# FFN gate and up by seven block products: a two-layer decoder step on one Trainium2 core

## The chip, the core and the metric

The kernel runs on one core of one Trainium2 chip (trn2). The metric is the device time of one execution in microseconds; a run is compared with other runs by the median. The engines are named as in the profile: PE is TensorE (matmul), PEld its weight loads, DVE is VectorE, ACT is ScalarE, POOL is GpSimd, SP is SyncE, whose queue here only issues DMAs.

## What is computed

One step of two layers over 1024 prompt tokens and 8 sample tokens (T = 1032 token columns), model width 1024, all in float32. Each layer is a token mixer (layer 0 an mLSTM, layer 1 a latent attention with a paged cache), an output projection added to the residual, and a SwiGLU FFN added to the residual; a last norm ends it. The part that the change touches:

```python
hp = hp + yp                                   # yp = (...) @ w_out, the output projection
hp = hp + swiglu(rmsnorm(hp, norm_ffn[layer]), ffn_w_gate_up[layer], ffn_w_down[layer])

def swiglu(x, w_gate_up, w_down):              # w_gate_up (1024, 2*2816), w_down (2816, 1024)
    g, u = jnp.split(x @ w_gate_up, 2, axis=-1)
    return (jax.nn.silu(g) * u) @ w_down
def rmsnorm(x, g):
    return x * lax.rsqrt(jnp.mean(x * x, axis=-1, keepdims=True) + EPS) * g
```

## The kernel before

Features lie on the 128 partitions and tokens along the free dimension, so an activation of width 1024 is a tile of 8 feature tiles (KT) by 1032 columns, cut into three chunks of 344 (CW). Every float32 operand of a large product is split into two float32r parts, high and low (`split`, L95: ScalarE copies the high part, VectorE or GpSimd subtracts it for the low one), and one product is three matmuls, high by high, high by low, low by high (`mm3`, L114). A weight block of 128 output features is loaded and split by `load_w` (L120), which has two raw tiles `wr` and two tiles each for the high and low part; `linear` (L138) then runs the three chunks, 8 contraction tiles and 3 terms each: 72 matmuls of 344 columns.

The instructions of each engine are put into an order when the kernel is built, by a scheduler that takes what is ready, earlier program lines first; at run time an engine works through its own list and waits on semaphores. SP's queue holds nearly all loads and stores in such an order, GpSimd's queue a few DMAs beside its arithmetic.

`out_proj` (L723 on) reads the residual X from DRAM (`x_d`) into one tile of 8 x 1032, and for each of 8 output tiles d adds the product of the projection to X and prepares the FFN's operands at once: X times the norm's gain, split, into `xz`, and the squares summed into `rs` (`prep`, L193). The 1/rms of a token is not yet in them. The first gate tile's products (`lead`) run while `rs_of` (L207) makes 1/rms.

`ffn` goes over 22 feature tiles f of the hidden width 2816 in groups of 5, 5, 4, 4, 4. For each f it runs the gate product and the up product, 144 matmuls of 344 columns; `ev_g` (L757) multiplies the gate by 1/rms on VectorE, takes Silu on ScalarE and multiplies by 1/rms again on GpSimd; `ev_u` (L764) multiplies and splits the activation (`ah`, `al`). After a group, the down product of its 4 or 5 tiles is added into X on chip, output tile by output tile (L779 to L786). In layer 0 the last group's down product also prepares the operands of the attention's projections (`to_mla` in `run`); in layer 1 `finish` (L1371) runs the last group's down product in three token ranges, transposes the rows and normalises them to the output. X stays on chip from `out_proj` to the end of the FFN.

The operands of the two projections, `z`, are made by `mlstm` (end, L436 to L444) and by `mla_out` (L1343) and `attention` (L1253 to L1255), each in three chunks of 344 columns.

Of the kernel before, what the change touches and what calls it, by code (L numbers as in the profile page):

```python
# [18 lines left out]
P = 128  # L19
# [11 lines left out]
NCK = S // L  # L31
QL = 384
# [5 lines left out]
# columns of the constant table  # L38
# [34 lines left out]

class Kern:
# [19 lines left out]
    # one exact split of a float32 array into two float32r parts  # L94
# [11 lines left out]
    # the same from PSUM, the low part on GpSimd  # L106
# [7 lines left out]
    def mm3(self, ps, wh, wl, xh, xl, start, stop):  # L114
        mm = self.nc.tensor.matmul
        mm(ps, wh, xh, start=start, stop=False)  # L116
        mm(ps, wh, xl, start=False, stop=False)  # L117
        mm(ps, wl, xh, start=False, stop=stop)  # L118
# [18 lines left out]
    # emit(c, columns, product) for each token chunk of x  # L137
# [10 lines left out]
    # few weight columns: both parts of w side by side, the low one from row o on  # L148
# [17 lines left out]
    # products whose results are used later, so that they run ahead  # L166
# [5 lines left out]
    # 1/sqrt(v) of a small tile: a first guess from the exponent, then Newton steps  # L172
    def rsqrt(self, pool, v, shape, tag):
        V = self.nc.vector
        y = self.t(pool, shape, tag + "y")
        u = self.t(pool, shape, tag + "u")
        V.tensor_scalar(y.bitcast(I32), v.bitcast(I32), 1, None, op0=ALU.logical_shift_right)
# [14 lines left out]
    # x*g split for one feature tile and chunk, and its squares  # L192
# [13 lines left out]
    # rs holds sums of squares per partition on entry, 1/rms on exit  # L206
# [14 lines left out]
    # ---------------------------------------------------------------- set-up  # L221
# [41 lines left out]

    def new_z(self, pool):
# [59 lines left out]
        # 1/rms per token, then as a row on every partition  # L324
# [18 lines left out]
    def mlstm(self, xz, rs, early):  # L343
# [11 lines left out]
        # gates: input gate rows at 0, forget gate rows at 32  # L355
# [42 lines left out]
        # sigmoid(o) * g = tanh(o / 2) * g / 2 + g / 2; the last term is added where it is used  # L398
# [37 lines left out]
        z = self.new_z(self.zp)  # L436
        pz = self.pool("mz")
        for c in range(NCH):
            cs = slice(c * CW, (c + 1) * CW)
            for h in range(8):  # L440
                og = self.t(pz, [P, CW], "og", bufs=6)
                nc.sync.dma_start(og, o_d[:, h, cs])
                nc.vector.scalar_tensor_tensor(og, og, self.gcol(self.G_HEAD + h), v[:, h, cs], op0=ALU.add, op1=ALU.mult)
                self.split(z[0][:, h, cs], z[1][:, h, cs], og, lo_eng=nc.gpsimd if h % 3 == 2 else None)  # L444
# [4 lines left out]
    def gates(self, p1, pg, gi, lf, bcol):  # L449
# [5 lines left out]
        # log sigmoid  # L455
# [4 lines left out]
        # sample gates kept  # L460
# [49 lines left out]
    # one chunk of four heads, as two parts: products, then norm and output  # L510
    def mlstm_chunk(self, pi, c, hg, q, k, v):
# [12 lines left out]
        # decay weights [s, t] per head  # L524
# [11 lines left out]
        # k with its weights, and [v | 1], token major  # L536
# [31 lines left out]
        # state  # L568
# [17 lines left out]
        # h / max(|den|, exp(-m)), then its norm, as one factor per token and head  # L586
# [17 lines left out]
    def mlstm_sample(self, pi, q, k, v):  # L604
# [35 lines left out]
        # weighted k, masked q: [p, b, hp]  # L640
# [5 lines left out]
        # normaliser  # L646
# [20 lines left out]
        # v rows  # L667
# [45 lines left out]
    # out projection into the residual, with the operands of the norm after it  # L713
    def out_proj(self, w, z, gbase, last=False):
        nc = self.nc
        if not last:
            self.fz = self.pool("fz")
        self.xpool = self.pool("xp")
        X = self.t(self.xpool, [P, KT, T], "x")
        self.nt = self.pool("nt")  # L720
        if last:
            self.fz = self.pool("fz")
        xz = self.new_z(self.fz)  # L723
        rs = self.t(self.fz, [P, T], "rs")
        for d in range(KT):
            (nc.gpsimd if last else nc.sync).dma_start(X[:, d], self.x_d[:, d])
# [9 lines left out]
        if last:  # L736
            self.p2.release()
# [772 lines left out]
```

## Time and profile before

| what | us |
|---|---|
| median of 3 runs | 2821.42 |
| lowest and highest run | 2818.59, 2833.71 |
| the profiled execution's span | 2830.2 |
| layer 0: mLSTM, to the first projection product | 0 to 432 |
| layer 0: projection, then FFN | 432 to 538, 538 to 1284 |
| layer 1: attention | 1284 to 1978 |
| layer 1: projection, then FFN | 1978 to 2070, 2070 to 2765 |
| last products and norm | 2765 to 2830 |

The profiled execution is one execution of its own, taken by the hardware profiler; its span is the time from its first to its last instruction. Busy time of TensorE is the union of matmuls that overlap, each some 0.3 us long, so the cost of one matmul in a stream is read from the spacing of the starts. The granted clock in the windows is a share of full speed (2.4 GHz).

### The profile page before, as it was taken

How to read it: one execution, taken by the hardware profiler on the slowest of the kernel's cores; microseconds unless marked ns; L12 is line 12 of the kernel's file. 1: busy time of each engine (PE TensorE's matmuls, PEld its weight loads, DVE VectorE, ACT ScalarE, POOL GpSimd, SP SyncE). 2: the span in 40 equal slices, each digit the busy share in tenths (PEclk: the TensorE clock that was granted, in tenths of full speed). 3: DMA queues.
4: the chain of work that ended last, by engine and by line, in shares of the span. 5: the costliest groups of instructions: out<-in, count | busy, mean ns of one | idle time of the engine just before them, and what ended most of it. 6: DMA issues, size and time to landing. Idle time of an engine off the chain costs nothing. (4 is left out here: it accounts for less than half of the span.)

```text
span 2830.2 us, 47930 instructions
## 1 busy us (share of the span) xinstructions
PE 2720.3 (96%) x19623; PEld 2555.6 (90%) x19623; DVE 1340.7 (47%) x2989; ACT 876.7 (31%) x2021; POOL 721.6 (25%) x729
## 2 busy tenths in 40 slices
PE   8998899999999999999879999999999999999998
PEld 8988888999999999999866666767999999999998
DVE  4366675423222223247668787778432223232324
ACT  4222234321211111243455555655321121212122
POOL 1001232230311121232334444442222120302023
PEclk9999899999999999999989999999999999999999
DMA  5132434111111121122567665663311111111112
GB/s 180 38 75 64 122 108 148 46 40 55 49 38 53 38 60 37 54 87 75 159 204 243 209 230 199 214 237 125 105 46 40 55 40 54 42 53 38 54 41 86
DMA packets 281840, 271.53 MB, mean 96 GB/s; under 512 B 18857, under 2 KB 258990, under 8 KB 273302
## 3 DMA queue, kind: packets, MB, share of 16 engines
q1 hardware_dynamic: 262854, 167.81, 20.0%
q0 software_dynamic: 18000, 98.56, 10.1%
q8 instruction: 154, 2.52, 0.4%
q10 hardware_dynamic: 768, 2.11, 0.3%
q14 instruction: 64, 0.52, 0.1%
HBM read 229.36 MB, written 36.97 MB: 94 GB/s over the span
## 5 line engine op out<-in xcount | busy, mean ns | idle before, releaser
L116 PE MATMUL sc<-zh,wh 128*128 128x344 f32 x2000 | 642.8, 322 | 5.5 <-ACT zh L99 4.9
L117 PE MATMUL sc<-zl,wh 128*128 128x344 f32 x2000 | 641.4, 321 | 1.2 <-DVE zl L100 0.6
L118 PE MATMUL sc<-zh,wl 128*128 128x344 f32 x2000 | 641.1, 321 | 1.1 <-DVE wl L100 1.1
L99 ACT ACTIVATE wh<-wr 128x1024 fp32r<-128x1024 f32 (+3 forms) x219 | 196.8, 899 | 731.0 <-PE mm L117 721.0
L116 PE MATMUL mm<-zh,wh 128*128 128x344 f32 x1192 | 385.4, 323 | 0.5 <-DVE ot L402 0.5
L116 PEld LDWEIGHTS sc<-zh,wh 128*128 128x128 f32 x2000 | 377.2, 189 | 9.1 <-ACT zh L99 5.1
L117 PE MATMUL mm<-zl,wh 128*128 128x344 f32 x1192 | 384.1, 322 | 0.4 <-POOL zl L100 0.4
L118 PE MATMUL mm<-zh,wl 128*128 128x344 f32 x1192 | 383.8, 322 | 0.0
L117 PEld LDWEIGHTS sc<-zl,wh 128*128 128x128 f32 x2000 | 376.8, 188 | 2.9 <-DVE zl L100 1.8
L118 PEld LDWEIGHTS sc<-zh,wl 128*128 128x128 f32 x2000 | 377.5, 189 | 1.8 <-DVE wl L100 1.6
L762 POOL TENSOR_TENSOR sg<-g,rs 128x344 f32<-128x344 f32 x132 | 144.8, 1098 | 782.0 <-ACT g L760 762.3
L100 DVE TENSOR_TENSOR wl<-wr,wh 128x1024 fp32r<-128x1024 f32 (+3 forms) x216 | 224.8, 1042 | 54.2 <-ACT wh L99 51.2
L100 POOL TENSOR_TENSOR al<-sg,ah 128x344 fp32r<-128x344 f32 x132 | 146.5, 1111 | 334.1 <-ACT ah L99 334.1
L117 PEld LDWEIGHTS mm<-zl,wh 128*128 128x128 f32 x1192 | 225.3, 189 | 2.4 <-issue 1.2
L116 PEld LDWEIGHTS mm<-zh,wh 128*128 128x128 f32 x1192 | 225.8, 189 | 1.3 <-DVE ot L402 0.8
L118 PEld LDWEIGHTS mm<-zh,wl 128*128 128x128 f32 x1192 | 225.8, 189 | 0.5 <-issue 0.5
L116 PE MATMUL sc<-ah,wh 128*128 128x344 f32 (+2 forms) x664 | 212.4, 320 | 0.0
L117 PE MATMUL sc<-al,wh 128*128 128x344 f32 (+2 forms) x664 | 212.2, 320 | 0.0
L118 PE MATMUL sc<-ah,wl 128*128 128x344 f32 (+2 forms) x664 | 212.1, 319 | 0.0
L1287 DVE STREAM_TRANSPOSE tt<-nat 128x1024 f32<-128x1024 f32 x128 | 156.4, 1229 | 15.1 <-PE ss L1291 10.2
L760 ACT ACTIVATE g<-g 128x344 f32<-128x344 f32 x132 | 64.4, 488 | 274.0 <-DVE g L759 273.0
L99 ACT ACTIVATE ah<-sg 128x344 fp32r<-128x344 f32 x132 | 64.3, 487 | 269.6 <-DVE sg L765 268.8
(470 smaller groups left out, 4717.9 us busy)
## 6 DMA issues: line engine op xcount, KB each, us to landing
wr<-in_ffn_w_gate_up_dram SPq DMA_DIRECT2D x88, 512.0 KB
wr<-in_mlstm_w_in_dram SPq DMA_DIRECT2D x24, 512.0 KB
wr<-in_ffn_w_down_dram SPq DMA_DIRECT2D x48, 256.0 KB
wr<-in_ffn_w_down_dram SPq DMA_DIRECT2D x32, 320.0 KB
q<-qn_d SPq DMA_DIRECT2D x32, 256.0 KB
qn_d<-qx SPq DMA_DIRECT2D x16, 344.0 KB
x_d<-x POOLq DMA_DIRECT2D x1, 4128.0 KB
o_d<-ot POOLq DMA_DIRECT2D x24, 172.0 KB, 4.6
```

The lines of the kernel that those rows point to most:

```text
L99: ins = nc.scalar.activation(hi, src, AF.Copy)
L100: e.tensor_tensor(lo, src, hi.bitcast(F32), op=ALU.subtract)
L116: mm(ps, wh, xh, start=start, stop=False)
L117: mm(ps, wh, xl, start=False, stop=False)
L118: mm(ps, wl, xh, start=False, stop=stop)
L760: nc.scalar.activation(g1, g1, AF.Silu)
L762: nc.gpsimd.tensor_tensor(sg[c], g1, rs[:, cs], op=ALU.mult)
L1287: V.transpose(out=tt, in_=src.rearrange("p s (c i) -> p c s i", i=32))
```

## The change

Gate and up of one f are taken as one product of a 2 x 2 block matrix. Weight blocks: a11, a12 are the even and odd contraction tiles of the gate's 128 columns, a21, a22 those of the up's. The tokens are cut into two halves of 512 and 520 columns (i = 0, 1), and each half into two blocks of 256 or 260 columns (PW); the even and odd feature tiles of a half by its two blocks are b11, b12, b21, b22. Seven block products (a variant of Strassen's scheme with 15 additions) replace the eight of the plain product. `PRODUCTS` lists them as (product, PSUM bank, first use of the bank): two banks take a second product by accumulation, the other sums are made when a bank is read.

`forms` makes the seven operands of a token half out of X: the 1/rms (`rms_tok`, `as_row`), X times gain times 1/rms in place, the four differences, and seven splits. `operands` makes the seven weight operands of an f: GpSimd adds, ScalarE and VectorE split 512 columns each. `gate_up` runs each product for both halves and evacuates. X is not kept: `out_proj` writes the residual to `x_d`, and `down` adds the down product of two f at a time to `x_d` with accumulating DMAs from GpSimd's queue (`accum_op`), out of a staging tile `st` with two buffers. Its chunks are drawn one by one between the products of `gate_up`. The projection runs for the first token half over all 8 output tiles (512 columns), then for the second (two pieces of 260), with its weights loaded for each; the first half's forms are drawn in while the second half runs. `to_mla` and `finish` read X from `x_d` again and do the last four f's down product.

```diff
+PW = (256, 260)
+PRODUCTS = ((0, "a", 1), (1, "b", 1), (4, "a", 0), (2, "c", 1), (5, "b", 0), (3, "d", 1), (6, "c", 0))
+BANK = {"a": "sc", "b": "sc", "d": "sc", "c": "mm"}
 def out_proj
-        X = self.t(self.xpool, [P, KT, T], "x")
+        X = [self.t(self.xpool, [P, KT, 2 * PW[i]], f"x{i}") for i in range(2)]
+        for i in range(2):
+            for d in range(KT):
+                wh, wl = self.w0 if layer and i == d == 0 else self.load_w(self.wsrc(w, 0, KT, d * P, P), KT, P)
+                m = 512 if i == 0 else PW[1]
+                for c0 in range(0, n, m):
+                    for k in range(KT):
+                        self.mm3(ps, wh[:, k], wl[:, k], zh[:, k, cs], zl[:, k, cs], k == 0, k == KT - 1)
+                    V.tensor_tensor(x, x, ps, op=ALU.add)
...
+                nc.sync.dma_start(self.x_d[:, d, cols[i]], X[i][:, d])
+                next(gen, None)
+            if i == 0:
+                self.zp0.release()
+                self.nf = self.pool("nf", side="right")
+                gen = self.forms(i, X[i], SS, self.G_FFN + 8 * layer)
...
+        for _ in self.forms(1, X[1], SS, self.G_FFN + 8 * layer):
+            pass
+def forms(self, i, X, SS, g0):
+        y = self.rms_tok(SS, n)
+        yield
+        self.as_row(y, rs, n)
+        B = X.rearrange("p (k r) (c t) -> p r c k t", r=2, c=2)
+        def normed(r):
+            for k in range(r, KT, 2):
+                V.scalar_tensor_tensor(X[:, k], X[:, k], self.gcol(g0 + k), rs, op0=ALU.mult, op1=ALU.mult)
...
+        normed(0)
+        put(0, B[:, 0, 0])
+        t1 = sub(B[:, 0, 1], B[:, 0, 0])
+        put(1, t1)
+        yield
+        normed(1)
+        put(4, B[:, 1, 0])
+        yield
+        put(2, sub(B[:, 1, 1], B[:, 0, 1]))
+        yield
+        t2 = sub(B[:, 1, 1], t1)
+        put(5, sub(t2, B[:, 1, 0]))
+        yield
+        put(3, t2)
+        put(6, B[:, 1, 1])
+def operands(self, wg, f):
...
+        G = nc.gpsimd.tensor_tensor
+        G(s, a21, a22, op=ALU.add)
+        G(s3, a11, a21, op=ALU.subtract)
+        yield put(a11)
+        yield put(s)
+        yield put(a12)
+        yield put(s3)
+        yield put(a22)
+        G(s, s, a11, op=ALU.subtract)
+        yield put(s)
+        G(s, s, a12, op=ALU.subtract)
+        yield put(s)
+def gate_up(self, wg, f, parts, down=iter(()), skip=0):
+        for (s, bank, first), w in zip(PRODUCTS, self.operands(wg, f)):
+            for i in parts:
+                for k in range(4):
+                    self.mm3(ps, w[:, 0, k], w[:, 1, k], xh[:, k], xl[:, k], bool(first) and k == 0, k == 3, ...)
+                if s == 0:
+                    nc.scalar.copy(u[:, 1], ps)
+                elif s in (1, 2, 3):
+                    V.tensor_tensor(u[:, 1], u[:, 1], ps, op=ALU.add)
+                elif s == 4:
+                    nc.scalar.activation(g[:, 0], ps, AF.Silu)
+                if s == 3:
+                    V.tensor_tensor(u[:, 0], u[:, 1], banks[i, "b"], op=ALU.subtract)
+                    V.tensor_tensor(u[:, 0], u[:, 0], g[:, 0], op=ALU.mult)
+                if s == 6:
+                    V.tensor_tensor(g[:, 1], u[:, 1], ps, op=ALU.subtract)
+                    nc.scalar.activation(g[:, 1], g[:, 1], AF.Silu)
+                    V.tensor_tensor(u[:, 1], u[:, 1], g[:, 1], op=ALU.mult)
+                    self.split(o(ah), o(al), u, lo_eng=nc.gpsimd)
+                if skip:
+                    skip -= 1
+                else:
+                    next(down, None)
+def down(self, wd, f0):
+        for d in range(KT):
+            raw = self.t(fp, [P, 2, P], "dr", bufs=2)
+            nc.sync.dma_start(raw, self.wsrc(wd, f0 * P, 2, d * P, P))
+            self.split(wh, wl, raw)
+            st = self.t(fp, [P, T], "st", bufs=2)
+            for c in range(NCH):
+                ps = self.tp()[:, :CW]
+                for j in range(2):
+                    self.mm3(ps, wh[:, j], wl[:, j], ah[:, cs], al[:, cs], j == 0, j == 1)
+                nc.scalar.copy(st[:, cs], ps)
+                if c == NCH - 1:
+                    nc.gpsimd.dma_start(self.x_d[:, d], st, accum_op=ALU.add)
+                yield
+def ffn(self, layer):
+        self.gate_up(wg, 0, (0,))
+        self.gate_up(wg, 1, (0, 1))
+        self.gate_up(wg, 0, (1,))
+        for f in range(2, NF - 2, 2):
+            g = self.down(wd, f - 2)
+            self.gate_up(wg, f, (0, 1), g, 4)
+            self.gate_up(wg, f + 1, (0, 1), g)
...
+        self.gate_up(wg, NF - 2, (0, 1))
+        for parts in ((0,), (1,)) if layer else ((0, 1),):
+            self.gate_up(wg, NF - 1, parts)
```

## Rows read from the trace of the kernel before

**Rows 1.** The table of cores: span and granted clock.
```profile
core 0: 2830.2 us, clock 0.983
```
**Rows 2.** The page, part 1: busy us, share of the span, instructions.
```profile
PE 2720.3 (96%) x19623; PEld 2555.6 (90%) x19623; DVE 1340.7 (47%) x2989; ACT 876.7 (31%) x2021; POOL 721.6 (25%) x729
```
**Rows 3.** Windows by stage: from:to, us, busy (instructions) by engine, PEclk, DMA share, GB/s.
```profile
core 0: us, PE busy (x) PEld busy (x) DVE busy (x) ACT busy (x) POOL busy (x), PEclk, DMA share, GB/s
437.00:538.00 101.00, 98.87 (x614) 96.51 (x614) 54.48 (x88) 39.21 (x74) 25.20 (x25) 1.00 0.34 109
538.00:562.00 24.00, 24.00 (x152) 22.64 (x151) 11.40 (x21) 7.82 (x14) 7.37 (x7) 1.00 0.15 45
562.00:1240.00 678.00, 678.00 (x4310) 678.00 (x4309) 189.56 (x298) 124.65 (x202) 138.28 (x125) 1.00 0.16 46
1985.00:2072.00 87.00, 87.00 (x559) 86.37 (x558) 37.95 (x54) 29.53 (x54) 21.01 (x21) 1.00 0.24 78
2072.00:2085.00 13.00, 13.00 (x80) 12.34 (x79) 7.57 (x18) 5.74 (x11) 3.44 (x4) 1.00 0.14 42
2085.00:2700.00 615.00, 615.00 (x3912) 615.00 (x3912) 175.53 (x274) 110.77 (x178) 122.51 (x111) 1.00 0.16 47
```
**Rows 4.** Timeline, VectorE in FFN 1: start us, us, instruction; first gate chunk, successive f.
```profile
2699.49 0.52 DVE L759 TENSOR_TENSOR g<-sc,rs 128x344 f32<-128x344 f32 x1 [1.61 <-PE sc L118]
...
2722.13 0.52 DVE L759 TENSOR_TENSOR g<-sc,rs 128x344 f32<-128x344 f32 x1 [1.61 <-PE sc L118]
```
**Rows 5.** Timeline, TensorE in the tail: first and last of 21 matmuls, two widths.
```profile
2796.73 0.34 PE L116 MATMUL sc<-ah,fw 128*128 128x384 f32 x1
...
2800.24 0.33 PE L118 MATMUL sc<-ah,fw 128*128 128x384 f32 x1
...
2812.92 0.28 PE L116 MATMUL sc<-ah,fw 128*128 128x264 f32 x1
...
2815.37 0.28 PE L118 MATMUL sc<-ah,fw 128*128 128x264 f32 x1
```
**Rows 6.** Groups by form, VectorE: form xcount, busy us, mean ns, idle before.
```profile
L100 DVE TENSOR_TENSOR wl<-wr,wh 128x1024 fp32r<-128x1024 f32 x130 | 160.7, 1236 | 46.2 <-ACT wh L99 46.2
...
L100 DVE TENSOR_TENSOR wl<-wr,wh 128x512 fp32r<-128x512 f32 x42 | 29.1, 693 | 0.2
...
L100 DVE TENSOR_TENSOR wl<-mm,wh 128x256 fp32r<-128x256 f32 x32 | 12.9, 403 | 2.1 <-ACT wh L99 1.8
L181 DVE TENSOR_TENSOR fu<-fu,ssq 128x4 f32<-128x4 f32 x48 | 9.3, 194 | 1.5
...
L1416 DVE SCALAR_TENSOR_TENSOR yo<-sc,r,gB 128x512 f32<-128x512 f32 x7 | 5.2, 748 | 0.1
```
**Rows 7.** Groups by form, ScalarE.
```profile
L760 ACT ACTIVATE g<-g 128x344 f32<-128x344 f32 x132 | 64.4, 488 | 274.0 <-DVE g L759 273.0
...
L99 ACT ACTIVATE wh<-wr 128x512 fp32r<-128x512 f32 x43 | 27.2, 633 | 158.5 <-PE mm L117 158.2 <-ACT rs L200 0.3
...
L1204 ACT COPY ot<-mm 128x256 f32<-128x256 f32 x28 | 10.4, 371 | 40.9 <-PE mm L1201 40.9
```
**Rows 8.** Groups by form, GpSimd.
```profile
L112 POOL TENSOR_TENSOR wl<-spl,wh 128x512 fp32r<-128x512 f32 x43 | 54.8, 1284 | 41.0 <-ACT spl L111 39.3 <-issue 1.1
```
**Rows 9.** Line 726, loads of x on GpSimd's queue: issue ns, landing us min/median/max.
```profile
L726 POOL DMA_DIRECT2D x<-x_d x8: 550/558/612, 1978.4 to 1982.1; - x8
...
DMA to landing us min/median/max: 4.8/9.8/10.9
```
**Rows 10.** Timeline, VectorE and GpSimd at the end of projection 0.
```profile
527.46 0.57 DVE L103 SCALAR_TENSOR_TENSOR zl<-x,g,zh 128x344 fp32r<-128x344 f32 x1 [0.65 <-ACT zh L102]
...
531.90 1.12 POOL L204 TENSOR_TENSOR rs<-rs,sq 128x344 f32<-128x344 f32 x1 [3.07 <-ACT sq L203]
...
532.14 1.24 DVE L103 SCALAR_TENSOR_TENSOR zl<-x,g,zh 128x344 fp32r<-128x344 f32 x1
```
**Rows 11.** Timeline, TensorE's first projection product in layer 0, idle before it.
```profile
432.30 0.66 PE L116 MATMUL sc<-zh,wh 128*128 128x344 f32 x1 [4.88 <-ACT zh L99]
```

More of the change, by code (lines that the diff above doesn't have):

```diff
@@ L71, in host_tables, with __init__, __getitem__ @@
     return c, r.astype(np.float32)
+class Stack:
+    def __init__(self, tiles):
+        self.tiles = tiles
+    def __getitem__(self, ix):
+        return self.tiles[ix[1]][:, ix[2]]
 class Kern:
@@ L219, in rs_of, with rms_tok, as_row @@
             nc.scalar.copy((rs if out is None else out)[:, j * QW:(j + 1) * QW], ps)
+    def rms_tok(self, SS, n):
+        nc = self.nc
+        c, rem = divmod(n, P)
+        ps = self.tp()
+        for i in range(c):
+            nc.tensor.matmul(ps[:, i:i + 1], SS[:, i * P:(i + 1) * P], self.ones[:, 0:1], start=True, stop=True)
+        v = self.t(self.gp, [P, 9], "tv")
+        w = c + (rem > 0)
+        if rem:
+            nc.gpsimd.memset(v[:, c:w], 1.0)
+            nc.tensor.matmul(ps[:rem, c:w], SS[:, c * P:n], self.ones[:, 0:1], start=True, stop=True)
+            nc.vector.tensor_scalar(v[:rem, c:w], ps[:rem, c:w], 1.0 / D, EPS, op0=ALU.mult, op1=ALU.add)
+        nc.vector.tensor_scalar(v[:, :c], ps[:, :c], 1.0 / D, EPS, op0=ALU.mult, op1=ALU.add)
+        return self.rsqrt(self.gp, v[:, :w], [P, 9], "t", w)
+    def as_row(self, y, out, n):
+        for c0 in range(0, n, 512):
+            ps = self.tp()
+            m = min(512, n - c0)
+            for i in range(0, m, P):
+                w = min(P, m - i)
+                t = (c0 + i) // P
+                self.nc.tensor.matmul(ps[:, i:i + w], y[:, t:t + 1].to_broadcast([P, P]), self.ident[:, :w], start=True, stop=True)
+            self.nc.scalar.copy(out[:, c0:c0 + m], ps[:, :m])
     def setup(self):
@@ L262, in gcol, with half_z @@
         return self.g[:, o:o + 1]
+    def half_z(self):
+        self.zp1 = self.pool("z1", side="right")
+        self.zp0 = self.pool("z0", side="right")
+        pools = (self.zp0, self.zp1)
+        return [[self.t(pools[i], [P, KT, 2 * PW[i]], "zh" + str(i) + x, F32R) for x in "hl"] for i in range(2)]
     def new_z(self, pool):
@@ L741, in ffn, with out_proj @@
[L741 removed]
+    def out_proj(self, w, z, layer):
         nc = self.nc
         V = nc.vector
[L744 to L790 removed]
@@ L1388, in finish @@
             W.append(tuple(w[:, i].rearrange("p (k m) -> p k m", m=P) for i in range(2)))
+        for cs in cuts[1:]:
+            for d in range(KT):
+                nc.sync.dma_start(X[d][:, cs], self.x_d[:, d, cs])
         gB = self.t(fp, [P, D], "gB")
@@ L1443, in finish @@
         fp.release()
+        self.fp.release()
+        self.fz.release()
     def run(self):
```

326 lines of the change are left out of this document (201 added, 125 removed).

## The prediction

> **What bounds the kernel now.** I read the table of cores first: one core, a span of 2830.2 us, a granted clock of 0.983 [rows 1]. The page's engine shares put TensorE at 96% and the next engine, VectorE, at 47% [rows 2]; a share over the whole span says little, so the windows by stage come next. In both FFN stretches TensorE is busy for all of the 678 and 615 us, at clock 1.00, VectorE for 28% of them, ScalarE for 18%, GpSimd for 20% [rows 3]. The two projection windows are 98% and 100% TensorE, and even the hand-over from projection to FFN has no gap: 24.0 of 24.0 and 13.0 of 13.0 us [rows 3]. So in the FFN a microsecond of matmul removed is a microsecond of the kernel, as long as no other engine becomes late.
>
> What one matmul costs is read from starts, not from the 0.32 us durations, which overlap. One feature tile of gate and up is 144 matmuls of 344 columns and comes round every 22.64 us [rows 4]: 157.2 ns each. In the tail, 21 matmuls of 384 columns start within 3.51 us and 21 of 264 columns within 2.45 us, each with 20 spacings: 175.5 and 122.5 ns [rows 5]. The line through these two has 0.442 ns per column and 5.9 ns fixed; it gives 157.8 at 344 columns (measured 157.2), 119.0 at 256, 120.7 at 260 and 232 at 512.
>
> **The change, part by part.**
>
> *Gate and up.* Removed: 22 tiles x 144 x 2 layers = 6336 matmuls at 157.2 ns, 996.2 us. Added: 7 products x 2 token halves x 4 contraction tiles x 3 split terms = 168 per tile, 7392 in all, half at 256 and half at 260 columns, mean 119.9 ns: 885.9 us. Net -110.3 us. Bounds: were a matmul strictly proportional to its columns (118 ns) it would be -124; were none under the 122.5 ns of the 264-column row, -91.
>
> *Down.* The same 1584 matmuls per layer, at 344 columns in the same three chunks, now two tiles deep for all but the last four: 0. In the steady loop one step is a product half (12 x 119.9 ns = 1.44 us) and one down chunk (6 x 157.2 = 0.94 us), so a pair of tiles takes 28 x 1.44 + 24 x 0.94 = 63 us. VectorE in a pair: 14 weight splits of 512 at 0.69, 28 small operations on a token half at about 0.42 (between the 0.40 of the 256-column row and 0.52 at 344), 8 splits of 256 at 0.40 [rows 4, 6]: 25 us, 39%. ScalarE: 14 x 0.63, 16 operations of 0.37 to 0.63, 24 copies of 0.49, 8 x 0.37 [rows 7]: 30 us, 48%. GpSimd: 8 sums and 4 splits of 512 at 1.28 [rows 8] and 8 DMA issues at 0.57 [rows 9]: 20 us, 32%. TensorE covers all three, so I book 0, with up to +20 for small waits at the finer hand-overs (three hand-overs where there was one).
>
> *Accumulating DMAs.* Each `down` step of one feature tile ends with a 516 KB accumulate issued by GpSimd; 72 per layer. No row shows an accumulate. The nearest are plain 516 KB reads on the same queue: 4.8 us for the quickest of eight in a burst, 9.8 us in the median, 10.9 us for the slowest [rows 9]. The staging tile `st` has two buffers, so a DMA has from the end of its third chunk to the end of the first chunk two tiles later, four steps, 9.5 us; the two PSUM banks of that helper give two steps more before TensorE itself waits, 14.3 us. An isolated plain transfer (one every 7.2 us here, not eight at once) is nearest to 4.8 us; doubled it is 9.6. Cost 0; what it costs beyond 14.3 us is rival C.
>
> *Hand-over from projection to FFN.* This is where the change pays. Before, gate products ran on unscaled operands while the 1/rms was still being made. Now the second token half needs X, its sum of squares, the 1/rms row, eight scalings, four differences and seven splits before its first product can end. TensorE's cover is the first half's pass of tile 0 (84 x 119 ns = 10.0 us) and then tile 1 with both halves (20.2 us). VectorE's work from the last projection product to the end of tile 1: about 3.4 us in the 1/rms chain (13 small operations at 0.19, two at 0.42), 8 scalings of 520 at 0.75, 11 operations of 1040 at 1.24, 12 weight splits of 512 at 0.69, 19 evacuations at 0.42 [rows 6]: 39 us against 30.2 us of matmul. So TensorE waits for at least 9 us. GpSimd adds to it: a VectorE operation that usually takes 0.57 us took 1.24 beside a GpSimd sum of 1.12 [rows 10], 0.67 more. Eleven GpSimd operations in this stretch, if each costs that once, make 7 us. I take 16 per layer, +32 in all; bounds +10 (work drawn ahead of the hand-over) and +50 (the forms go first on VectorE and the weights starve).
>
> The Trainium skill, "SBUF — State Buffer", section "SBUF: two separate sides", says more: VectorE operations with two SBUF inputs and GpSimd operations hold one port pair in turn, and the loser blocks for the whole instruction. The rows just cited agree in kind. By that rule all 11 x 1.28 = 14 us of GpSimd work would be lost to VectorE, 23 us per layer, and the time would be some 14 us higher (rival B).
>
> *Projection by halves.* 192 matmuls at 232 ns and 384 at 120.7 against 576 at 157.2: 90.9 against 90.5 us, 0. While the second half runs (46 us), VectorE has the first half's forms (8 x 0.75 + 11 x 1.24 = 19.6), 16 residual adds at 0.42 and 8 weight splits at 1.24 (the weights are now loaded twice) [rows 6]: 36 us, plus GpSimd collisions. It fits in sum but comes in lumps of up to 7 us against 5.8 us of matmul; the next weight split stands behind them on VectorE, and TensorE waits for it: +3 per layer, +6 (0 to +16). The first product now needs 512 instead of 344 columns of z from VectorE; before it TensorE already sat idle 4.9 us [rows 11]. Eight times 0.17 us more, scaled up by the splits: +1.5 per projection, +3 (-2 to +6, below nothing as the longer first product covers more). The stores of X go on SP's queue between the weight loads; each waits for a residual add, with the next weight already loaded: 0.
>
> *One-half passes* (tile 0 in two passes in both layers, the last tile in two passes in layer 1): weight forms made once more per 10 us pass, VectorE 7 x 0.69 + 7 x 0.42 = 7.8 us [rows 6], so only collisions can make it late: +4 (0 to +10). *Ends:* reading X back from DRAM before the last products, 3 KB to 4 KB rows on SP's queue among the weights: the last accumulate was issued some 40 us earlier, and reads of tiles other than the last fit under the last pass: +2 (0 to +8). Layer 0's end, with the same matmuls and x read instead of held: +1 (0 to +4).
>
> **Sum.** -110.3 + 32 + 6 + 3 + 4 + 2 + 1 = -62. The profiled execution's own span, 2830.2 us, lies 0.3% over the median of the runs, 2821.4, and inside their 2818.6 to 2833.7; I apply the difference to the median: 2759 us.
>
> **The rivals.**
>
> *A. The hand-overs are hidden.* The forms are drawn ahead and the stalls keep to their low bounds: -110 + 10 + 5 = -95, 2726 us. For it: TensorE has no gap there today [rows 3]. Against: 39 us of VectorE work in 30 us.
>
> *B. VectorE and GpSimd are late.* Each GpSimd operation of the hand-over costs VectorE its whole 1.28 us (14 us on top of the 9), and forms that go first hold back the weights for some 7 more: hand-over 30 per layer, projection 8 per layer by the same collisions, steady loop +10: -110 + 60 + 16 + 10 + 10 (the other small terms) = -14, 2807 us. For it [rows 10]; against, shares of 39% and 32% in the steady loop.
>
> *C. The accumulating DMA becomes the bound: slower.* Place: the `st` buffer in the steady loop. Each us beyond 14.3 delays every second feature tile by one, 72 x 2 / 2 = 72 us over the kernel. It cancels the gain at about 15.2 us, and at twice the median landing of that burst (2 x 9.8 = 19.6 us) it costs +380: about 3140 us; just past the point, at 16.5 us, it gives 2821 - 62 + 158 = 2917. For it: no row prices an accumulate, which reads, adds and writes DRAM. Against: the lone plain landing of 4.8 us [rows 9], the DMA engines only 16% busy in the FFN [rows 3], and 9.5 us until the first effect.
>
> *D. The change does not do what it says:* the pitch at 256 columns sticks at 122.5 ns or above. That is -91 instead of -110, 2778 us, inside the forecast's own range.
>
> **How the numbers follow.** Forecast (with D) 0.51, own range 2738 to 2790; A 0.19; B 0.17; C 0.13. The predicted time is the forecast's, 2759. The range reaches from A's side (gate and up at -110 with low bounds of the rest, about -103: 2718) to beyond B (2815), and leaves out C and the far end of A. A measurement of this kernel can tell about 0.5% from no change, 14 us. Faster by more: the forecast, A and half of B, 0.78. Within: the rest of B, 0.09. Slower: C, 0.13.
>
> **What the profile after would show.** Gate and up right: TensorE matmuls of 256 and 260 columns at a spacing of 119 to 121 ns, 3696 each, and a pair of tiles every 63 us with TensorE full. Hand-over right: TensorE idle 10 to 25 us within the 30 us after the projection's last product in each layer, its waits ended by VectorE (low halves of forms or weights), the clock perhaps falling there. Accumulate right: landings under 10 us, no ScalarE copy to `st` waiting for a DMA. Rival B shows as VectorE near 100% through the second projection half; rival C as gaps of TensorE repeated every 14 us, ScalarE waiting on the DMA of `st`. The forecast is wrong if the steady loop takes more than 66 us a pair, or if the hand-overs cost under 5 or over 25 us each.

## The result, and the profile after

The changed kernel takes 2795.4 us (median of 4 runs, 2784.6 to 2797.4), the kernel before 2826.3 us beside it: ratio 0.988, interval 0.985 to 0.991. That is faster by 1.2%, 31 us, half of the 62 us forecast and inside the range. The profiled execution has a span of 2795.7 us against 2830.2 [rows 1], 34.5 us less.

The page's engine shares after (busy us, share of the span, instructions), and below it the windows by stage (columns as in [rows 3]): the projection of layer 0, four stretches of its FFN, then the same for layer 1.

```profile
PE 2631.5 (94%) x20739; PEld 2446.1 (87%) x20739; DVE 1588.1 (57%) x3542; ACT 1209.0 (43%) x2855; POOL 926.8 (33%) x887
```

```profile
426.90:536.60 109.70, 99.10 (x595) 87.91 (x596) 71.52 (x94) 41.18 (x62) 30.73 (x24) 0.94 0.55 173
536.60:562.00 25.40, 5.60 (x35) 5.31 (x35) 21.05 (x36) 10.65 (x15) 2.58 (x3) 0.58 0.22 62
562.00:580.00 18.00, 16.95 (x124) 16.66 (x124) 12.71 (x21) 8.45 (x17) 8.45 (x6) 0.83 0.15 45
580.00:600.00 20.00, 18.71 (x156) 18.50 (x156) 12.96 (x23) 7.55 (x16) 7.90 (x7) 1.00 0.23 65
600.00:1200.00 600.00, 600.00 (x4612) 600.00 (x4611) 254.69 (x484) 264.37 (x586) 219.52 (x192) 1.00 0.57 114
1941.40:2052.30 110.90, 104.80 (x627) 92.91 (x627) 63.52 (x94) 41.00 (x71) 38.25 (x41) 0.93 0.53 168
2052.30:2080.00 27.70, 6.44 (x37) 5.82 (x37) 23.31 (x37) 10.80 (x15) 1.26 (x1) 0.57 0.19 57
2080.00:2100.00 20.00, 19.38 (x152) 19.38 (x153) 12.85 (x21) 9.91 (x19) 9.72 (x7) 0.91 0.23 65
2100.00:2700.00 600.00, 598.65 (x4599) 598.44 (x4598) 252.78 (x487) 263.95 (x584) 220.24 (x193) 1.00 0.57 115
```

The steady loop is as full as before: 600.0 of 600.0 us. Where [rows 3] had 24.0 of 24.0 in the hand-over from projection to FFN there are now 5.6 of 25.4, at a granted clock of 0.58, with VectorE busy 21.05. The projections, 98% to 100% TensorE before, have holes of 10.6 and 6.1 us.

From here on a projection is the time from its first product on z to the start of its last residual add, and an FFN from there to the first product of what follows (the operands z of layer 1's attention, "MLA" in the code, or the last down product), read from the starts of these instructions. By these marks the projections of the kernel before run from 432.3 to 530.1 and from 1961.9 to 2058.7 us; the table of the kernel before sets their ends and the second one's start later, at 538, 2070 and 1978, but TensorE is just as full between (31.94 of 31.94 us from 530.06 to 562).

| kernel | ratio to before | projection 0 / 1, us | FFN 0 / 1, us |
|---|---|---|---|
| before | 1 | 97.8 / 96.8 | 750.5 / 704.7 |
| changed | 0.988 (0.985 to 0.991) | 109.7 / 110.9 | 719.4 / 679.3 |
| e1_order | 0.987 (0.985 to 0.989) | 111.1 / 115.0 | 718.1 / 675.8 |
| e2_one_form | 0.979 (0.976 to 0.981) | no trace used | no trace used |
| e3_lo_gpsimd | 0.990 (0.988 to 0.993) | 109.5 / 107.7 | 725.2 / 682.7 |
| e4_plain_store | 0.989 (0.987 to 0.991) | 109.4 / 109.4 | 719.1 / 679.3 |
| e5_proj_order | 0.990 (0.988 to 0.993) | 112.7 / 110.4 | 719.1 / 678.7 |
| e7_one_form_both | 0.973 (0.970 to 0.975) | 104.9 / 99.9 | 708.4 / 666.5 |
| e8_eighth_product | 1.031 (1.028 to 1.033) | 111.2 / 108.3 | 779.3 / 737.8 |
| e9_no_gpsimd | 0.990 (0.988 to 0.993) | 112.0 / 113.7 | 719.5 / 679.3 |
| e11_lag | 0.984 (0.982 to 0.986) | 107.8 / 110.2 | 716.3 / 673.8 |
| e14_deep_weights | 0.985 (0.983 to 0.987) | 106.3 / 105.5 | 719.1 / 678.8 |
| e15_lag_deep | 0.983 (0.981 to 0.985) | 105.9 / 107.1 | 715.5 / 673.9 |
| e16_spread_x | 0.979 (0.977 to 0.981) | 101.6 / 105.3 | 716.2 / 672.2 |

The kernel before took 2826 to 2828 us beside e1 to e5, e14 and e15, and 2852 to 2860 us beside e7, e8, e9, e11 and e16, so only ratios and stages are compared across. An FFN that an edit leaves alone repeats within 0.7 us (the changed kernel, e5, e9 and e14: 719.1 to 719.5 and 678.7 to 679.3); a projection left alone scatters by 3 to 4 us (107.8 to 111.2 and 107.7 to 110.9 in the changed kernel, e3, e4, e8 and e11). Of e2 only the times of undisturbed executions are used.

The 34.5 us, stage by stage: FFNs -31.1 and -25.4, projections +11.9 and +14.1, the way to the first projection product -5.4, MLA +4.1, the tail -2.7.

In the hand-over of layer 0, the one long wait of TensorE, and what ScalarE and VectorE did before it (timeline of the changed kernel: start us, us, engine, instruction, idle before and what ended it; L936 copies the first product out of PSUM, L112 and L113 are the high and low parts of a split):

```profile
561.12 0.58 PE L129 MATMUL sc<-f4h,wl 128*128 128x256 f32 x1 [16.71 <-ACT u L936]
...
559.74 1.07 ACT L112 ACTIVATE c5h<-T 128x1040 fp32r<-128x1040 f32 x1 [1.23 <-DVE T L844]
560.72 0.35 ACT L936 COPY u<-sc 128x256 f32<-128x256 f32 x1
...
544.91 3.44 DVE L840 SCALAR_TENSOR_TENSOR x<-x,g,rs 128x520 f32<-128x520 f32 x5 [2.91 <-ACT rs L261]
548.27 1.24 DVE L844 TENSOR_TENSOR T<-x 128x1040 f32<-128x1040 f32 x1
...
561.93 1.24 DVE L113 TENSOR_TENSOR c5l<-T,c5h 128x1040 fp32r<-128x1040 f32 x1
```

TensorE has done one product of tile 0 and needs its copy u to go on; ScalarE makes that copy behind the last of the second half's seven high copies, and these come as VectorE delivers the scaled X and the differences, from 544.9 to 563 us without a gap. So two readings were open: the order is wrong (ORDER: copy and weight splits behind the forms), or VectorE has too much to do (THROUGHPUT).

### The profile page after: what moved, and what is told of

Same layout as the page of the kernel before. It is cut to its first block, busy times and chain, and to the rows that moved or that the text cites. A ratio compares the mean times of both kernels' runs of the same rounds, so it can differ in the third digit from the quotient of the medians.

```text
span 2795.7 us, 52716 instructions
## 1 busy us (share of the span) xinstructions
PE 2631.5 (94%) x20739; PEld 2446.1 (87%) x20739; DVE 1588.1 (57%) x3542; ACT 1209.0 (43%) x2855; POOL 926.8 (33%) x887
## 5 line engine op out<-in xcount | busy, mean ns | idle before, releaser
L971 ACT COPY st<-ss 128x344 f32<-128x344 f32 x432 | 190.5, 441 | 208.4 <-PE ss L131 193.7
L131 PE MATMUL ss<-ah,dl 128*128 128x344 f32 x864 | 277.2, 321 | 0.0
L130 PE MATMUL ss<-al,dh 128*128 128x344 f32 x864 | 276.2, 320 | 0.0
L129 PE MATMUL ss<-ah,dh 128*128 128x344 f32 x864 | 276.0, 319 | 0.0
L112 ACT ACTIVATE wh<-wr 128x512 fp32r<-128x512 f32 (+2 forms) x152 | 119.8, 790 | 223.3 <-PE mm L130 127.2
L973 POOL DMA_DIRECT2D x_d<-st x144 | 125.2, 869 | 228.9 <-ACT st L971 219.3
L113 POOL TENSOR_TENSOR al<-u,ah 128x512 fp32r<-128x512 f32 (+1 forms) x88 | 124.2, 1411 | 156.9 <-ACT ah L112 156.8
L113 DVE TENSOR_TENSOR wh<-S,wh 128x512 fp32r<-128x512 f32 x95 | 84.2, 888 | 159.6 <-ACT wh L112 108.4
L129 PEld LDWEIGHTS ss<-ah,dh 128*128 128x128 f32 x864 | 162.8, 188 | 0.0
L130 PEld LDWEIGHTS ss<-al,dh 128*128 128x128 f32 x864 | 162.5, 188 | 0.0
L131 PEld LDWEIGHTS ss<-ah,dl 128*128 128x128 f32 x864 | 162.3, 188 | 0.0
L113 DVE TENSOR_TENSOR wl<-S,wl 128x512 fp32r<-128x512 f32 x93 | 68.2, 734 | 112.8 <-ACT wl L112 85.8
L1539 PEld LDWEIGHTS ss<-tt,qbd 128*32 128x32 f32 x2560 | 70.8, 109 | 43.3 <-DVE tt L1535 12.8
L113 DVE TENSOR_TENSOR wl<-wr,wh 128x1024 fp32r<-128x1024 f32 (+2 forms) x80 | 88.4, 1109 | 35.3 <-ACT wh L112 32.7
L113 DVE TENSOR_TENSOR dl<-dr,dh 128x256 fp32r<-128x256 f32 x144 | 76.7, 533 | 55.0 <-ACT dh L112 55.0
L129 PE MATMUL mm<-zh,wh 128*128 128x344 f32 x320 | 106.3, 332 | 0.2 <-DVE ot L451 0.2
L131 PE MATMUL mm<-zh,wl 128*128 128x344 f32 x320 | 105.3, 329 | 0.0
```

What stands on the lines that cost most here:

```text
L112: ins = nc.scalar.activation(hi, src, AF.Copy)
L113: e.tensor_tensor(lo, src, hi.bitcast(F32), op=ALU.subtract)
L129: mm(ps, wh, xh, start=start, stop=False, **kw)
L130: mm(ps, wh, xl, start=False, stop=False, **kw)
L131: mm(ps, wl, xh, start=False, stop=stop, **kw)
L971: nc.scalar.copy(st[:, cs], ps)
```

## The experiments

**The hand-over: order, or VectorE.** First the order alone; tile 0's buffers got a pool of their own:

```diff
-        for _ in self.forms(1, X[1], SS, self.G_FFN + 8 * layer):
+        gen = self.forms(1, X[1], SS, self.G_FFN + 8 * layer)
+        self.gate_up(wg, 0, (0,), gen)
+        for _ in gen:
             pass
```

> Only the order of issue is changed, in both layers: the seven first-half products of tile 0, with their weight splits and evacuations, are issued interleaved with the forms of the second half instead of behind them (their buffers lie in a pool of their own). Theory ORDER: the 22 to 25 us that TensorE now stands idle behind the projection are idle because the first copy of a product to SBUF and the weight splits queue on ScalarE and VectorE behind the forms; the half pass (84 products of 0.12 us, 10.1 us) then runs inside that stretch: 10 us less per layer, about 2775 us, and the wait of 16.7 us for the copy u is gone. Rival THROUGHPUT: VectorE has some 22 us of forms to do in any order, and the half pass puts about 11 us more of splits and additions between them; only the 8 us of the 1/rms chain, in which VectorE is half idle, is won: 0 to 7 us per layer, 2782 to 2795 us, with TensorE idle in pieces instead of in one block.

Measured: 2791.1 us, 4 us less, which is inside the scatter of the runs; the FFNs gain 1.3 and 3.5 us, but in the same trace the projections are 1.4 and 4.1 us longer. Windows of layer 0 from the last residual add on:

```profile
540.60:555.00 14.40, 12.47 (x90) 11.96 (x89) 13.17 (x26) 7.22 (x13) 6.79 (x6) 0.88 0.45 137
555.00:575.00 20.00, 2.14 (x17) 1.93 (x16) 18.79 (x24) 9.18 (x11) 0.78 (x1) 0.68 0.03 8
```

The half pass now runs at once, and the hole comes behind it: 17.9 of 20 us, with VectorE at 18.79. The long wait for u is gone and its time is not. This speaks for THROUGHPUT, but its sign (TensorE idle in pieces) is not there, and an order on another engine is not ruled out. The one long wait ends with the split of tile 1's first weights, and in ScalarE's list that split stands behind tile 0's last evacuation, for which ScalarE waits 3.4 us (timeline of e1, TensorE and ScalarE):

```profile
574.71 0.58 PE L129 MATMUL sc<-f0h,wh 128*128 128x256 f32 x1 [17.86 <-ACT wh L112]
...
572.57 0.42 ACT L958 ACTIVATE gt<-gt 128x256 f32<-128x256 f32 x1 [3.38 <-DVE gt L957]
...
574.05 1.13 ACT L112 ACTIVATE wh<-wr 128x512 fp32r<-128x512 f32 x2
```

The next edit gives GpSimd a part of VectorE's work:

```diff
-            self.split(F[s][0], F[s][1], x)
+            self.split(F[s][0], F[s][1], x, lo_eng=nc.gpsimd if i and s in (1, 2, 3) else None)
```

> Three of the seven low parts of the second half's forms are computed by GpSimd instead of VectorE; order unchanged. Theory ORDER: the copy u still stands behind the last high copy, at most 3 us per layer less, 2789 to 2796 us. Rival THROUGHPUT: VectorE loses 3 x 1.4 us of its row of forms and the last high copy comes as much earlier: 4 to 5 us per layer less, 2785 to 2788 us. Rival COLLISION (GpSimd and VectorE slow each other): no gain or a loss, 2795 us or more.

Measured: 2799.8 us; the FFNs lose 5.8 and 3.4 us. Two VectorE operations of 1.24 us beside GpSimd's low parts (timeline, layer 0):

```profile
558.91 3.42 DVE L113 TENSOR_TENSOR f7l<-x,f7h 128x1040 fp32r<-128x1040 f32 x1
562.25 3.41 DVE L844 TENSOR_TENSOR T<-T,x 128x1040 f32<-128x1040 f32 x1
...
558.51 2.71 POOL L113 TENSOR_TENSOR c2l<-T,c2h 128x1040 fp32r<-128x1040 f32 x1 [4.33 <-ACT c2h L112]
561.19 3.37 POOL L113 TENSOR_TENSOR c3l<-T,c3h 128x1040 fp32r<-128x1040 f32 x1
```

Each ends 1.1 us after the GpSimd operation beside it, about its own length: the rows read as if it waited for the end of that one. GpSimd takes 2.7 to 3.4 us for what VectorE does in 1.24, so the trade loses: COLLISION. This is what the Trainium skill, "SBUF — State Buffer", section "SBUF: two separate sides", says of the port pair that VectorE and GpSimd share: the one that starts first holds it for its whole instruction and the other waits. These rows agree with it.

What the forms cost in all was priced by leaving them out (part of the computation: one form stands in for seven; four scalings, four differences and six splits are not done), first in the second half, then in both:

```diff
         put(0, B[:, 0, 0])
+        if i:              # e7: in both halves
+            for s in range(1, 7):
+                F[s] = F[0]
+            return
```

> Leaves out part of the computation: of the second half's seven forms only the first is made, and it stands in for the other six (four normalised tiles, five differences, six splits per layer are not done). It prices the forms of the second half whole. If the missing part of the FFN's gain lies in the hand-over: 18 to 25 us per layer less than the changed kernel, 2745 to 2760 us, and the windows behind the projection fill up. If it lies elsewhere (a longer product, the accumulating DMA, the clock in the steady loop): less than 5 us per layer, over 2785 us.

> Leaves out part of the computation: of the seven forms of both halves of the tokens only the first is made, and it stands in for the other six. Against the run in which only the second half's forms were cut (2760 to 2767 us) it prices the forms of the first half, which are made during the second half of the projection. Theory THROUGHPUT (VectorE has more work than time there, about 18 us of forms beside the weight splits): the gap of 3.6 to 4 us behind the middle of each projection and the stretch at a lower clock behind it are gone, 4 to 6 us per layer less than that run, 2752 to 2758 us. Rival: these gaps come from the weight loads or from the order of the weight splits alone: within 3 us of that run.

Measured: 0.979 and 0.973. Against the changed kernel the second half's forms cost 0.0094 x 2826 = 27 us, 13 per layer, less than the 18 to 25 expected; the first half's another 16 us, 8 per layer, more than the 4 to 6 expected. The intervals of the ratios leave some 10 us either way on both. The stages of e7 say the same: FFNs -11.0 and -12.8, projections -4.8 and -11.0 (against e8's, beside the same runs of the kernel before, -6.3 and -8.4). A window in its second projection half, and then the same window and one in the first half of the changed kernel:

```profile
505.00:525.00 20.00, 20.00 (x170) 20.00 (x169) 8.79 (x13) 8.02 (x13) 8.34 (x8) 1.00 0.41 126
```

```profile
505.00:525.00 20.00, 16.38 (x122) 15.97 (x120) 19.38 (x21) 8.96 (x13) 6.55 (x6) 0.91 0.27 86
440.00:450.00 10.00, 3.02 (x10) 1.81 (x9) 10.00 (x12) 4.61 (x7) 3.05 (x3) 0.76 0.92 289
```

The last edit here takes work off VectorE's path: tile 0 in one pass over both halves, with the second half's products two weight combinations behind and one form issued between, so the second pass with its seven splits falls away:

```diff
-        self.gate_up(wg, 0, (0,))
         self.gate_up(wg, 1, (0, 1))
-        self.gate_up(wg, 0, (1,))
+    def first_tile(self, wg, gen):     # called with forms(1) as gen, ahead of ffn
+        for (s, bank, first), w in zip(PRODUCTS, self.operands(wg, 0)):
+            self.product(s, bank, first, w, 0, banks)
+            self.evacuate(s, bank, 0, banks, 0, U, Gt)
+            next(gen, None)
+            ...                        # product of half 1, two combinations behind
```

> The first tile of gate/up is done in one pass over both halves, issued together with the second half's forms: the second half's product of each weight combination follows two combinations behind the first half's, one form of the second half is issued between them, and tile 0's separate second-half pass, with its reload and splits of the weights, falls away. VectorE's work on the path shrinks by that pass (7 splits of 0.69 us and its additions), and 20 us of products lie beside the 19 us of forms in place of none. If VectorE's throughput is what binds, this should give 8 to 12 us per layer, 2771 to 2779 us; if the latency from form to form and the order on ScalarE bind instead, less than 3 us per layer, 2789 us or more.

Measured: 0.984, the FFNs 3.1 and 5.5 us shorter; half of what was expected, and in neither theory's range. From the last residual add to 600 us TensorE idles 14.9 us where the changed kernel idled 22.1. The edit changes work and order at once, so it does not tell the two apart. The two longest waits that stay, each in both layers, are for the first form and again for the split of tile 1's weights on ScalarE, of the kind that the rival named (timeline of e11, layer 0):

```profile
555.36 0.58 PE L130 MATMUL sc<-c0h,wl 128*128 128x260 f32 x1 [4.30 <-ACT c0h L113]
...
583.88 0.39 PE L130 MATMUL sc<-f0h,wh 128*128 128x256 f32 x1 [3.79 <-ACT wh L113]
```

**The projections.** A first try at order: weights issued ahead of the forms' next piece, finer pieces, the loads of x spread.

```diff
+                w1 = weights(i * KT + d + 1)
                 nc.sync.dma_start(self.x_d[:, d, cols[i]], X[i][:, d])
-                if i == d == 0:
-                    load(1)
+                if i == 0:
+                    (nc.gpsimd if layer else nc.sync).dma_start(X[1][:, d], self.x_d[:, d, cols[1]])
                 next(gen, None)
```

> Only the projections are changed: the weights of a step are split before the forms' next piece is issued and not behind it, the first two steps' weights of layer 0 ahead of the second half of z, the second half of x is loaded one block per step instead of eight blocks at once, and the forms of the first half come in finer pieces. Theory ORDER: the gaps of the two projections (7 and 4 us in layer 0, 2 and 4 us in layer 1, and the stretches at half clock behind them) are weight splits queued on VectorE behind z or forms, and weight loads behind x loads: 8 to 12 us per layer less, 2771 to 2780 us. Rival: VectorE or the DMA engines are full in these stretches whatever the order: less than 3 us per layer, over 2789 us.

Measured: 2800.1 us, no gain. This does not decide against ORDER: the timeline of e5 says that the edit could not act. In layer 0's first half only the first two steps' splits had been put ahead of z, and TensorE waited 5.46 us for the third's, as before. In the second half, weights have two buffers, so the split of a step waits for TensorE to leave the buffer of two steps before, and by then the lump is on VectorE:

```profile
504.81 1.06 ACT L112 ACTIVATE wh<-wr 128x1024 fp32r<-128x1024 f32 x1 [0.60 <-PE sc L130]
...
506.46 2.61 DVE L853 SCALAR_TENSOR_TENSOR x<-x,g,rs 128x512 f32<-128x512 f32 x3
508.99 1.21 DVE L113 TENSOR_TENSOR wl<-wr,wh 128x1024 fp32r<-128x1024 f32 x1
```

Then GpSimd's share of the projections given to VectorE:

```diff
-                self.split(z[i][0][:, h], z[i][1][:, h], og, lo_eng=nc.gpsimd if h % 3 == 2 else None)
+                self.split(z[i][0][:, h], z[i][1][:, h], og)
...
-                        (V if d == KT - 1 else nc.gpsimd).tensor_tensor(SS[:, cs], SS[:, cs], sq, op=ALU.add)
+                        V.tensor_tensor(SS[:, cs], SS[:, cs], sq, op=ALU.add)
... (and the same for the z of layer 1)
```

> In the two projections the low parts of z and the sums of squares that GpSimd computes are given to VectorE; nothing else is changed. Theory COLLISION (VectorE stands still while GpSimd computes, so a low part of 512 columns costs 1.35 to 1.5 us of both where VectorE alone takes 0.69): the stall of 7 us at the start of layer 0's projection shrinks by 3 to 5 us, and layer 1's stages by 1 to 3 us: 2785 to 2791 us. Rival: VectorE is the engine that is full and gets more to do: 2796 to 2803 us.

Measured: 0.990, projections 112.0 and 113.7 us: no gain, as the rival had it. The collisions there cost no more than the work would on VectorE. Then the buffers:

```diff
+        self.w3 = self.pool("w3", bufs=2, side="right")
...
+                while len(Q) <= min(j + (3 if i else 0), 2 * KT - 1):
+                    Q.append(weights(len(Q)))
```

> Only the projections' weights are changed: three steps' weights in layer 0 are split ahead of the second half of z, and in the second half of both projections the weights are split up to four steps ahead in two more pairs of buffers, ahead of the first half's forms. VectorE's work is the same. If the gaps in the projections are lumps (VectorE has enough time over the whole stage, 37 us of work in the 48 us of the second half, but the splits that TensorE needs come behind 20 us of forms), buffers cure them: 5 to 9 us per layer less than the changed kernel, ratio to the kernel before 0.981 to 0.984. If VectorE is full over the whole stage, the gap only moves to the next stage: within 2 us per layer, ratio 0.986 to 0.990.

Measured: 0.985, 9 us less than the changed kernel; projections 3.4 and 5.4 us shorter. The same window of the second half:

```profile
505.00:525.00 20.00, 20.00 (x169) 20.00 (x168) 20.00 (x23) 10.76 (x15) 7.26 (x6) 1.00 0.34 109
```

VectorE is full for all 20 us and TensorE is too. So this gap was a lump and not a lack: the splits lay behind the forms, and buffers cure it. What stays is in the first half (layer 0: TensorE waits 3.9 us for one split, then 2.5 us for another). With both edits that helped (e15), ScalarE waits for a weight in layer 1:

> Both edits that leave VectorE's work on the path smaller or earlier: tile 0 of gate/up in one pass issued together with the second half's forms (ratio to the kernel before 0.984 alone), and the projections' weights split further ahead. If the two gaps are separate lumps of the same engine the gains add: ratio 0.976 to 0.981, faster than both kernels. If VectorE is full over the whole stretch from the projection to the second tile, the second edit brings nothing on top: 0.983 to 0.986.

```profile
1955.16 1.06 ACT L113 ACTIVATE wh<-wr 128x1024 fp32r<-128x1024 f32 x1 [13.09 <-DMA wr<-in_mla_w_o_dram]
```

Measured: 0.983, faster than both kernels. As a ratio this is less than the sum of the two (0.981) and lies in the range for "nothing on top", but by stages the two do add: the FFNs are as short as e11's, the projections, within their scatter, as e14's. The 13.1 us is the wait of ScalarE; TensorE loses 3.2 us of it. The expectation of the next run places that load behind the eight blocks of x. In layer 0 the blocks do stand before the weights in SP's queue, but in layer 1 they go through GpSimd's queue, and the load only runs beside them, with the DMA engines 95% busy or more from 1935 to 1955 us. That expectation's 100.0 us for projection 1 also leaves out its first 7 us; from its first product it takes 107.1. The last run spreads the blocks:

```diff
-                if i == d == 0:
-                    load(1)
+                if i == 0:
+                    (nc.gpsimd if layer else nc.sync).dma_start(X[1][:, d], self.x_d[:, d, cols[1]])
```

> The kernel with the one-pass first tile and the weights split ahead, with one more edit: the second half of x is loaded one block per step of the first half, not eight blocks behind the first step, and the first half's weights are loaded one step further ahead. In the run without it the weight loads of steps 3 and 4 stand behind the eight blocks of x (ScalarE waits 13.1 us for one in layer 1, TensorE stands 2.7 to 3.9 us at a time, the DMA engines over 95% busy). If that queue is the rest of the projections' excess (105.9 and 100.0 us against 97.8 and 96.8 before), each layer gains 2 to 5 us more: ratio 0.980 to 0.982. If VectorE's second half of z is what holds TensorE there, no change: 0.983.

Measured: 0.979 (2798.8 us where the kernel before took 2859.6; interval 0.977 to 0.981), the lowest ratio of a kernel that leaves nothing out: 2.1% faster than before. Projection 0 is 4.3 us shorter than in e15. Projection 1 is 1.8 us shorter, which is inside the scatter, and this was on a chip whose MLA was slower (706 us against 678 in e15, unedited in both), so what the spreading does in layer 1 stays open.

**The two terms taken for certain.** An eighth product, without use:

```diff
                 if s == 0:
+                    px = self.tp()[:, :pw]
+                    for k in range(4):
+                        self.mm3(px, w[:, 0, k], w[:, 1, k], xh[:, k], xl[:, k], k == 0, k == 3, skip_group_check=True)
```

> Adds work without use: in each pass the first block product is computed a second time into a spare bank that nobody reads, so that there are eight products again, with 12 x 2 x 22 x 2 = 1056 more products of 256 or 260 columns. If TensorE sets the pace of the FFN all through, each costs its 0.12 us: 127 us more than the changed kernel, about 2922 us, and seven products in place of eight are worth as much. Rival: in part of the FFN something else sets the pace (VectorE, the accumulating DMAs, the weights' loads) and the added products fall into its idle time: less than 100 us more, under 2895 us.

Measured: 0.0427 x 2826 = 121 us more than the changed kernel; by stages 59.9 and 58.5 us per FFN for 528 matmuls, 111 to 113 ns each. At the forecast's 119.9 ns they would be 63.3 us, so TensorE sets the pace except for 3 to 5 us per FFN; that these fell into the hand-over's hole is likely and not shown. And the store without accumulation (the sums then don't reach the residual):

```diff
-                    nc.gpsimd.dma_start(self.x_d[:, d], st, accum_op=ALU.add)
+                    nc.gpsimd.dma_start(self.dump_d[:, d], st)
```

> Leaves out part of the computation: the DMAs of the down products store them to another place in DRAM in place of adding them to the residual there; same bytes sent, no reading back by the DMA. It prices the accumulation. Theory: the accumulating DMAs are hidden (landing 5.6 us in the median against a budget of 9.5 to 14 us, 11 us of waits for their buffers in the whole run, and those beside a full TensorE): within 8 us of the changed kernel (ratio to the kernel before 0.985 to 0.991). Rival: accumulation slows the weights' loads or holds ScalarE's copies so that it is part of what is missing of the gain: 10 us or more less (ratio under 0.984).

Measured: 0.989, FFNs 719.1 and 679.3 us: the accumulation costs nothing.

## Why the prediction was right or wrong

**Gate and up, -110: right.** Starts of the first and last of 12 matmuls of 256 columns, and of one and the same subtraction in successive pairs of tiles (timelines of the changed kernel, TensorE and VectorE):

```profile
750.93 0.28 PE L129 MATMUL sc<-f3h,wl 128*128 128x256 f32 x1
...
752.23 0.28 PE L131 MATMUL sc<-f3h,wl 128*128 128x256 f32 x1
```

```profile
727.78 0.42 DVE L945 TENSOR_TENSOR gt<-u,mm 128x256 f32<-128x256 f32 x1 [0.54 <-PE mm L131]
...
790.61 0.42 DVE L945 TENSOR_TENSOR gt<-u,mm 128x256 f32<-128x256 f32 x1 [0.54 <-PE mm L131]
```

1.30 us over 11 spacings is 118.2 ns (119.0 from the line through [rows 5]); a pair takes 62.83 us (63). Rival D falls.

**Down and accumulation, 0: right.** All landings of the accumulating DMAs (us, minimum, median, maximum):

```profile
DMA to landing us min/median/max: 5.2/5.6/9.0
```

The estimate from [rows 9], nearer 4.8 than 9.8, held against the 9.5 us budget; e4 shows it from the other side. Rival C falls.

**Hand-over, +16 per layer: the step that failed, by half.** An FFN with seven products at full pace would be 55.2 us shorter, 695.3 and 649.5 us; measured 719.4 and 679.3: 24 and 30 us lost per layer against 16 and about 2 for the half passes. Layer 1's loss is over the 25 us that the prediction set as a sign of being wrong. Up to 600 us the windows hold 22.1 us of idle time in layer 0, and the granted clock is lower there (0.58 and 0.83). Two windows from the last residual add to the end of tile 1, layer 0 and layer 1, and one of the forms in layer 0:

```profile
536.60:593.70 57.10, 36.25 (x272) 35.66 (x272) 41.73 (x70) 22.69 (x37) 16.13 (x13) 0.76 0.21 61
2052.30:2109.80 57.50, 35.62 (x271) 35.01 (x272) 42.69 (x70) 22.70 (x37) 14.81 (x11) 0.76 0.21 60
...
545.00:563.00 18.00, 1.65 (x6) 1.35 (x6) 17.96 (x19) 8.58 (x10) 0.00 (x0) 0.50 0.15 44
```

The mechanism was named (39 us of VectorE's work against 30.2 us of products), and the work was sized rightly: 42 to 43 us. What failed is the overlap. The sum let the 30.2 us of products run beside it, so that the stretch would last as long as VectorE's work; it lasted 57 us. Of the cover only one product, 1.4 us, had run when the forms began, and nearly all the rest ran behind them. The 1/rms chain also counts by its length, 8.3 us from the last residual add to the first scaling, and not by the 3.4 us of VectorE's work in it. The 7 us for collisions have no place in the forms: GpSimd did nothing in those 18 us. My upper bound, "the forms go first on VectorE and the weights starve", was the case. Rival B's price of 30 per layer was nearer than mine, but not for its main reason, GpSimd's operations.

Moving the half pass alone gained next to nothing (e1): its splits and evacuations need the engine that was full. Without six of the seven second-half forms 11 to 13 us return (e7). The other 13 to 17 us, the chain, the one form left and the half passes, were not taken apart, and how much a better order of tile 1's weights would give was not tested.

**Projections, +3 lumps and +1.5 first product per layer: right in kind, short in size.** Measured +11.9 and +14.1. The lumps were there, with VectorE at 19.38 of 20 us from 505 to 525; rival B's sign, VectorE near 100% through the whole second half, was not (39.2 of 53.8 us, near the 36 of the sum). I priced them at the split's own delay; leaving out the forms gives 4.8 and 11.0 us per layer (e7), splitting the weights earlier 3.4 and 5.4 (e14). What I did not have is the first half: in layer 0 the making of z's second half keeps VectorE busy for all of 440 to 450 us, so a weight split comes 5.5 us late; and in layer 1 a weight load issued at 1955.3 us, beside the loads of x, took 7.8 us to land where the median is 4.3. "The stores of X ... 0" looked at the stores and not at the loads of x, of which the change puts the second half, in layer 0, between the weight loads on SP's queue. The sum had no term for the clock either: of layer 1's 14.1 us only 6.1 are holes, and for the rest TensorE is busy, at a granted clock of 0.67 in the first 8.6 us (1941.4 to 1950) and 0.93 over the projection.

**Small terms.** The tail (-2.7 where +2 stood) and the start (-5.4) came out better, MLA 4.1 us worse; none was followed up, and the 4 us that they give together are luck.

**The rivals.** A falls with the hand-over. B has VectorE late in hand-over and projection, as it was, but puts it down to GpSimd's operations, which e9 and the window of the forms do not bear out, and its +10 for the steady loop is not there: TensorE lost 0 and 1.4 us of 600. The time lies between the forecast and B.

## What to carry to other kernels

When a scheme cuts matmul work by adding sums of operands, price the sums where they are made, not where they are used: the loop gained its 110 us, and some 43 us went back (e7) at the two places per layer where one engine makes all operands of the next stage at once. A cover of matmuls counts only as far as they need nothing from the engine that is late. And a lump in front of a short wait wants a deeper buffer before another order of issue: with two buffers the reordering could not act, with four, and the splits issued further ahead, the same engine, full in that window, held up nobody there.

## What the runs showed of the hardware

An accumulating DMA of 516 KB from GpSimd's queue took 5.2 us at the least and 5.6 in the median, and 0.87 us to issue; the plain store of the same bytes (e4) 2.9 and 3.6, and 0.56 to issue:

```profile
DMA to landing us min/median/max: 2.9/3.6/6.2
```

So the accumulation adds 2.0 us to a landing, which I had only bounded. GpSimd is no second VectorE: beside a GpSimd operation of 2.7 us a VectorE operation of 1.24 us took 3.4 (e3). And here an idle TensorE paid twice. Around and after the wait of 5.5 us in projection 0 the granted clock of 445 to 450 us is 0.52, close to the lower of its two levels (1.2 of 2.4 GHz), and matmuls of 512 columns start 0.43 us apart where they later start 0.23 to 0.24 apart:

```profile
448.47 0.79 PE L131 MATMUL mm<-zh0h,wl 128*128 128x512 f32 x1 [5.46 <-DVE wl L113]
449.06 0.63 PE L129 MATMUL mm<-zh0h,wh 128*128 128x512 f32 x1
449.49 0.63 PE L130 MATMUL mm<-zh0l,wh 128*128 128x512 f32 x1
...
456.93 0.40 PE L129 MATMUL sc<-zh0h,wh 128*128 128x512 f32 x1
457.17 0.40 PE L130 MATMUL sc<-zh0l,wh 128*128 128x512 f32 x1
```
